# The last feed-forward block's first projection: seven block products per pair of hidden tiles instead of eight

## The chip, the cores and the metric

One core of a Trainium2 chip runs the whole kernel. The metric is the device time of one execution in microseconds (us). Times inside a profile count from the start of its span. The engines are TensorE (PE in the profile; its weight loads are PEld), VectorE (DVE), ScalarE (ACT), GpSimd (POOL) and SyncE (SP), which starts the DMAs.

## The reference

One inference step of a two-layer audio encoder: 512 new prompt frames and 8 streams of 16 frames, 640 columns in all, with 1024 features. Layer 0 is a convolution module and a feed-forward block, layer 1 attention and a feed-forward block. All is float32. What the change touches is the feed-forward block of layer 1:

```
def swiglu_ffn(h, g, w_in, w_out):
    a, b = jnp.split(rms_norm(h, g) @ w_in, 2, axis=-1)
    return h + (jax.nn.silu(a) * b) @ w_out
```

`w_in` is 1024 x 5632 (hidden size 2816, for `a` and for `b`), `w_out` is 2816 x 1024. A last `rms_norm` follows and gives the output.

## The kernel before

Features lie on the 128 partitions and frames along the columns. `h` holds 8 feature tiles (k = 0 to 7) of 640 columns; the columns are worked on in two groups, `GR`: 0 with 256 columns, 1 with 384. A float32 operand is split into a high part (ACT copies it, rounded) and a low part (DVE subtracts the high part), and each product takes three matmuls: high weight by high x, low weight by high x, high weight by low x (`mm3`, lines 161 to 163). Weights are split by `wsplit` (DMA at lines 125 and 130, ACT `whi` at 141, DVE or POOL `wlo` at 145), activations by `xsplit` (ACT at line 150, DVE at line 151).

The block in question is at the end of the program. `rms_late` multiplies `h` by the norm's gain (DVE, line 243) and splits the result; the norm's factor per column (`bc`) is worked out beside it (squares on ACT at 168, their sum on POOL at 184, column means on PE at 193, the power on POOL at 218, the spread over partitions on PE at 205, the copy on ACT at 250) and is multiplied in only after the projection. `ffn` then goes over the 22 hidden tiles in the three chunks of `F1` (9, 9 and 4). For each tile j, `ffn_in` loads 128 x 2048 weights (the tile of `a` and the tile of `b`) and runs for each column group two sums of 8 x 3 matmuls: 96 matmuls of 256 or 384 columns for a pair of tiles. Lines 278 to 281 multiply by `bc`, take the silu (ACT) and the product, and `xsplit` writes `hid`. After each chunk `ffn_out` adds that chunk's part of the second projection to `h` (DVE, line 291). In the last chunk of 4 tiles all of group 1's columns are done first and then all of group 0's, so that the final norm of group 1 (lines 876 to 886) runs beside the matmuls of group 0. Ahead of the block stands the last attention projection, `proj_o(3)`, whose results DVE adds to `h` at line 694.

The order on each engine is set by the framework's scheduler, which places the operations by its own estimate and by priorities (`tc.high_priority`); each engine then runs its row of instructions strictly in that order.

## Time and profile before

| what | value |
|---|---|
| median of 3 runs | 1572.6 us (1569.3 to 1572.96) |
| profiled execution, its own time | 1573.84 us |
| its span, first to last instruction | 1572.1 us |
| mean granted TensorE clock | 0.984 |
| PE busy | 1497.4 us, 95% of the span |
| DVE, ACT, POOL busy | 970.1, 605.0 and 396.8 us |

The profiled execution took 1.2 us more than the median, and its span is 1.7 us shorter than its own time. Busy times are sums over stages with different limits: the last stage, from about 1085 us to the end, is the one to read here. A row of a group gives the line, the engine and the operation, what it writes and reads, the shape, the count, busy time and mean duration of one, and the idle time ahead of it with the engine it waited for.

### The profile page before, as it was taken

To read this page: it belongs to the slowest core of one execution; us is meant where nothing else is said; L and a number is where in the kernel's file an instruction comes from. 1 tells how busy PE (TensorE), PEld (TensorE's weight loads), DVE (VectorE), ACT (ScalarE), POOL (GpSimd) and SP (SyncE) were. 2 spreads that over 40 slices of the span, in tenths; PEclk is the share of its full clock that TensorE was granted. 3 is DMA by queue.
4 is the path that set the end of the run, shared out by engine and by line. 5 is a ranking of instruction groups with operands and counts; after the bars stand their busy time and mean duration, and the time that the engine had idled before them with its cause. 6 is when DMAs were issued, how large, how long until landed. Compare 5 with 4: busy or idle time off the path is not lost.

```text
span 1572.1 us, 26820 instructions
## 1 busy us (share of the span) xinstructions
PE 1497.4 (95%) x10998; PEld 1426.5 (91%) x10998; DVE 970.1 (62%) x1781; ACT 605.0 (38%) x1064; POOL 396.8 (25%) x368
## 2 busy tenths in 40 slices
PE   5888998989999999999999999998999999999997
PEld 5878888888999999999987898876999999999997
DVE  6994999988545545456776668575744334443345
ACT  4544454545433323235654345442522112221223
POOL 6864568877501000004221111011300000000001
PEclk9999999999999999999999999998999999999999
DMA  7884344444412333434655554450121232212311
GB/s 238 233 241 125 126 129 147 153 166 145 148 57 81 121 124 117 148 114 131 222 180 168 174 190 153 155 194 28 64 72 58 70 103 79 81 46 76 108 54 67
DMA packets 58700, 199.98 MB, mean 127 GB/s; under 512 B 10193, under 2 KB 22737, under 8 KB 45777
## 3 DMA queue, kind: packets, MB, share of 16 engines
q1 hardware_dynamic: 58288, 197.96, 39.1%
q8 instruction: 86, 1.41, 0.4%
q10 hardware_dynamic: 288, 0.31, 0.1%
q14 instruction: 38, 0.30, 0.1%
HBM read 187.02 MB, written 11.22 MB: 126 GB/s over the span
## 4 chain that ended last, share of the span: by engine, by line
PE 74%; DVE 15%; POOL 3%; issue 3%; ACT 2%; DMA 2%; SPq 0%; POOLq 0%; ACTq 0%; DVEq 0%
PE mm L161 22%; PE mm L162 22%; PE mm L163 22%; DVE w L425 5%; DVE wlo L145 4%; PE w L780 1%; DVE xl L151 1%; DMA x<-sc 1%; PE am L765 1%; POOL y L405 1%; PE am L748 1%; ACT whi L141 1%; PE am L811 1%; PE mm L457 1%; DVE hid L151 1%
## 5 line engine op out<-in xcount | busy, mean ns | idle before, releaser
L162 PE MATMUL mm<-xh,wlo 128*128 128x256 f32 (+1 forms) x2048 | 633.7, 311 | 14.9 <-DVE wlo L145 14.5
L161 PE MATMUL mm<-xh,whi 128*128 128x256 f32 (+1 forms) x2048 | 630.2, 311 | 8.2 <-ACT xh L150 3.7
L163 PE MATMUL mm<-xl,whi 128*128 128x256 f32 (+1 forms) x2048 | 630.0, 310 | 0.8 <-DVE xl L151 0.6
L162 PEld LDWEIGHTS mm<-xh,wlo 128*128 128x128 f32 x2048 | 390.8, 191 | 18.1 <-DVE wlo L145 17.0
L161 PEld LDWEIGHTS mm<-xh,whi 128*128 128x128 f32 x2048 | 388.5, 191 | 13.1 <-ACT xh L150 6.7
L163 PEld LDWEIGHTS mm<-xl,whi 128*128 128x128 f32 x2048 | 388.8, 191 | 3.0 <-DVE xl L151 1.9
L141 ACT ACTIVATE whi<-raw 128x2048 fp32r<-128x2048 f32 (+3 forms) x140 | 235.1, 1682 | 331.9 <-PE mm L163 269.4
L145 DVE TENSOR_TENSOR wlo<-raw,whi 128x2048 fp32r<-128x2048 f32 (+6 forms) x140 | 262.3, 1876 | 77.6 <-ACT whi L141 76.2
L162 PE MATMUL mm<-hid,wlo 128*128 128x384 f32 (+1 forms) x704 | 215.7, 308 | 6.7 <-DVE wlo L145 6.7
L163 PE MATMUL mm<-hid,whi 128*128 128x384 f32 (+1 forms) x704 | 213.5, 306 | 0.1
L161 PE MATMUL mm<-hid,whi 128*128 128x384 f32 (+1 forms) x704 | 212.1, 306 | 0.0
L145 POOL TENSOR_TENSOR wlo<-raw,whi 128x1536 fp32r<-128x1536 f32 (+3 forms) x50 | 145.1, 2905 | 70.4 <-ACT whi L141 70.4
L280 DVE TENSOR_TENSOR t<-mm,bc 128x384 f32<-128x384 f32 x66 | 33.8, 513 | 186.5 <-PE mm L163 186.5
L162 PEld LDWEIGHTS mm<-hid,wlo 128*128 128x128 f32 x704 | 132.3, 188 | 8.1 <-DVE wlo L145 8.1
L163 PEld LDWEIGHTS mm<-hid,whi 128*128 128x128 f32 x704 | 131.8, 188 | 0.5 <-DVE hid L151 0.3
L161 PEld LDWEIGHTS mm<-hid,whi 128*128 128x128 f32 x704 | 131.2, 188 | 0.2
L218 POOL TENSOR_TENSOR rst<-rst,mhalf 128x2 f32<-128x2 f32 (+1 forms) x7 | 6.0, 864 | 447.4 <-DVE rst L214 447.4
L291 DVE TENSOR_TENSOR h<-mm,h 128x384 f32<-128x384 f32 (+1 forms) x112 | 53.8, 485 | 102.7 <-PE mm L163 102.5
L425 DVE SCALAR_TENSOR_TENSOR w<-gp,dwv,w 128x384 f32<-128x384 f32 x180 | 103.8, 611 | 0.8
L279 ACT ACTIVATE t<-t 128x384 f32<-128x384 f32 x66 | 32.3, 490 | 157.0 <-DVE t L278 157.0
L150 ACT ACTIVATE hid<-t 128x384 fp32r<-128x384 f32 (+1 forms) x88 | 40.7, 462 | 117.2 <-DVE t L281 83.4
L184 POOL TENSOR_TENSOR acc<-sq,sq 128x384 f32<-128x384 f32 (+1 forms) x9 | 9.2, 1025 | 267.2 <-ACT sq L168 267.1
(154 smaller groups left out, 1897.7 us busy)
## 6 DMA issues: line engine op xcount, KB each, us to landing
raw<-in_w_in SPq DMA_DIRECT2D x62, 1024.0 KB
raw<-in_w_pw SPq DMA_DIRECT2D x22, 1024.0 KB
raw<-in_w_out SPq DMA_DIRECT2D x24, 768.0 KB
cache<-in_ck SPq DMA_DIRECT2D x32, 512.0 KB
cache<-in_cv SPq DMA_DIRECT2D x32, 512.0 KB
raw<-in_w_out SPq DMA_DIRECT2D x16, 576.0 KB
raw<-in_w_kq SPq DMA_DIRECT2D x8, 1024.0 KB
x<-sc SPq DMA_DIRECT2D x16, 368.0 KB
```

The costliest lines, as they stand in the source:

```text
L141: nc.scalar.activation(out=hi[:, a:b], in_=raw[:, a:b], func=AF.Copy)
L145: eng.tensor_tensor(out=lo[:, a:b], in0=raw[:, a:b], in1=hi[:, a:b].bitcast(F32), op=ALU.subtract)
L150: nc.scalar.activation(out=hi, in_=src, func=AF.Copy)
L151: nc.vector.tensor_tensor(out=lo, in0=src, in1=hi.bitcast(F32), op=ALU.subtract)
L161: nc.tensor.matmul(ps, wh, xh, start=(i == 0), stop=False)
L162: nc.tensor.matmul(ps, wl, xh, start=False, stop=False)
L163: nc.tensor.matmul(ps, wh, xl, start=False, stop=(i == last))
L279: nc.scalar.activation(out=s[:, :n], in_=s[:, :n], func=AF.Silu)
L280: nc.vector.tensor_tensor(out=t[:, :n], in0=ps[1], in1=bc, op=ALU.mult)
L291: nc.vector.tensor_tensor(out=hp(g, m), in0=pt[:, :n], in1=hp(g, m), op=ALU.add)
L405: nc.gpsimd.tensor_tensor(out=y[g][:, c, :], in0=y[g][:, c, :], in1=pr[:, :n], op=ALU.add)
L425: nc.vector.scalar_tensor_tensor(out=dst, in0=src, scalar=wj, in1=dst, op0=ALU.mult, op1=ALU.add)
```

## The change

In all but the first three pairs of hidden tiles the first projection is done by a block scheme with seven products. The 640 columns are cut into two halves of 320 (`TH`), the 1024 features into two halves of four tiles. With `A11`, `A12` for the weights of `a` and `A21`, `A22` for those of `b`, and `B` for the four blocks of x, four sums of weights (S1 to S4) and four of x (T1 to T4) are formed, and seven products of 12 matmuls with 320 columns each give both halves of `a` and `b`: 84 matmuls for a pair. The products are accumulated in three banks (`pa`, `pb`, `pc`): a product is copied out by ACT (`u`, `v`) and added into another bank by DVE (in `m6`), and later products accumulate on top of that.

* The weight sums are formed in place in `raw`, 512 columns each, two on DVE and two on POOL (`WE = "vpvp"`). 3584 columns of weights are split for a pair instead of 2048.
* The x blocks must hold the norm's factor before they are summed, so ACT writes the gained x (`xg`), the first three pairs run plainly on it (`plain`, four sums of 24 matmuls with 320 columns), and meanwhile DVE multiplies the blocks by the factor (`bca`), forms T1 to T4 and, with ACT, splits all seven blocks into 1280 columns each (`put`). `B11` and `B21`, `B22` and `T4` take the places of the plain x, `B22` and `T4` only after the third pair's last matmuls.
* The pairs are interleaved: the first, fifth, sixth and second product of the next pair stand between the seventh, third and fourth of the present one.
* The chunks of the second projection are 6, 6, 5 and 5 tiles (each chunk: 8 output tiles of both column groups), and in each chunk the two column groups alternate. The second projection's arithmetic is as before.
* `proj_o(3)` works on column halves instead of the two groups. Elsewhere only buffers are merged or named anew: ahead of `proj_o(3)` the rows of all engines stand as they did, but for some places at the end of layer 0 and the start of attention, where a few neighbours swap.

In the whole program 228 matmuls fall away: 19 pairs times 12.

Three places in the rows of the engines, before and now. Names end in a number for the buffer. First DVE in the middle of the first projection. Before, the work for one pair of tiles: scaling, product and low part for both groups, and one split of weights.

```order
L278 TENSOR_TENSOR t_1749_13612<-mm_13562,bc_11627 128x384
L280 TENSOR_TENSOR t_1750_13613<-mm_13587,bc_11627 128x384
L281 TENSOR_TENSOR t_1750_13613<-t_1749_13612,t_1750_13613 128x384
L151 TENSOR_TENSOR hid_13310<-t_1750_13613,hid_13310 128x384
L278 TENSOR_TENSOR t_1753_13670<-mm_13620,bc_11696 128x256
L280 TENSOR_TENSOR t_1754_13671<-mm_13645,bc_11696 128x256
L281 TENSOR_TENSOR t_1754_13671<-t_1753_13670,t_1754_13671 128x256
L145 TENSOR_TENSOR wlo_13802<-raw_13800,whi_13801 128x2048
L151 TENSOR_TENSOR hid_13311<-t_1754_13671,hid_13311 128x256
```

Now, from the end of one pair's fourth product on: `t` is the gate product, `bk` and `wlo` the low parts of weights, `raw` the weight sums, `pb` and `pc` the additions in the banks, `acc` the copy-out after the seventh product.

```order
L907 TENSOR_TENSOR t_1694_13187<-t_1683_13095,pb_13068 128x320
L159 TENSOR_TENSOR bk_13224<-raw_13220,bk_13224 128x512
L159 TENSOR_TENSOR hc_12850<-t_1694_13187,hc_12850 128x320
L907 TENSOR_TENSOR raw_13220<-raw_13220 128x512
L907 TENSOR_TENSOR pb_13191<-pb_13191,acc_13115 128x320
L907 TENSOR_TENSOR pc_13143<-pb_13191,sq_13144 128x320
L159 TENSOR_TENSOR wlo_13346<-raw_13343,whi_13345 128x1024
L159 TENSOR_TENSOR wlo_13223<-raw_13220,whi_13222 128x1024
L907 TENSOR_TENSOR raw_13343<-raw_13343 128x512
L907 TENSOR_TENSOR acc_13264<-pb_13191,sq_13144 128x320
L159 TENSOR_TENSOR bk_13224<-raw_13220,bk_13224 128x1024
L907 TENSOR_TENSOR t_1706_13293<-t_1706_13293,acc_13264 128x320
```

Nine operations for a pair have become thirteen, and two of them write the banks on which the next products accumulate.

Second ACT, where the first pairs are under way. Before, from the norm's factor on (`bc` to the next weights):

```order
L250 ACTIVATE bc_11627<-w_1544_11593 128x384
L279 ACT_TABLE_LOAD
L279 ACTIVATE t_1586_11756<-t_1586_11756 128x384
L150 ACTIVATE hid_11698<-t_1587_11757 128x384
L141 ACTIVATE whi_11945<-raw_11944 128x2048
L250 ACTIVATE bc_11696<-w_1567_11664 128x256
L279 ACTIVATE t_1590_11814<-t_1590_11814 128x256
```

Now, some microseconds later, around the start of the products: `x0f`, `x1f` and `xe` are high parts of x blocks (here of `B21`, `B22` and T2), `whi_12055` the weights of the first pair that is done by products (its second half holds S1 and S2), `acc_12079` the copy of its first product.

```order
L158 ACTIVATE x0f<-xg 128x1280
L158 ACTIVATE hc_11563<-t_1564_11862 128x320
L158 ACTIVATE x1f<-xg 128x1280
L158 ACTIVATE whi_12139<-raw_12137 128x1024
L158 ACTIVATE xe<-tq 128x1280
L158 ACTIVATE hc_11563<-t_1568_11920 128x320
L158 ACTIVATE whi_12055<-raw_12053 128x1024
L936 ACTIVATE t_1574_11983<-t_1574_11983 128x320
L910 ACTIVATE acc_12079<-pa_12078 128x320
L936 ACTIVATE t_1578_12045<-t_1578_12045 128x320
L1029 ACTIVATE t_1589_12135<-pa_12078 128x320
```

The high part of S1 and S2 now stands behind `B22` and T2 in ACT's row.

Third DVE at the end of the program. Before, where group 1's sums of squares (`acc_15651`) end and group 0's begin:

```order
L291 TENSOR_TENSOR h<-mm_15522,h 128x384
L184 TENSOR_TENSOR acc_15651<-acc_15651,sq_15670 128x384
L291 TENSOR_TENSOR h<-mm_15536,h 128x256
L291 TENSOR_TENSOR h<-mm_15550,h 128x256
L184 TENSOR_TENSOR acc_15688<-sq_15686,sq_15689 128x256
L291 TENSOR_TENSOR h<-mm_15564,h 128x256
L214 TENSOR_SCALAR rst_15676<-w_1929_15648 128x3
```

Now:

```order
L192 TENSOR_TENSOR acc_15688<-acc_15688,sq_15704 128x384
L1067 TENSOR_TENSOR h<-pc_15630,h 128x256
L1067 TENSOR_TENSOR h<-pa_15647,h 128x384
L192 TENSOR_TENSOR acc_15688<-acc_15688,sq_15707 128x384
L1067 TENSOR_TENSOR h<-pb_15664,h 128x256
L192 TENSOR_TENSOR acc_15724<-sq_15722,sq_15725 128x256
L222 TENSOR_SCALAR rst_15713<-w_1942_15685 128x3
```

Before, five of group 0's eight tiles are still to be added when group 1's mean (`rst`) is taken; now the last tiles of both groups are added first, and group 0's sum begins behind them.

The diff, cut to what the steps speak of:

```
+HT = 320
...
+TG = (slice(0, 256), slice(256, 640))
+TH = (slice(0, HT), slice(HT, 2 * HT))
...
-F1 = ((0, 9), (9, 9), (18, 4))
+F1 = ((0, 6), (6, 6), (12, 5), (17, 5))
+CH = 6
+NPL = 3
+WE = "vpvp"
...
-        return (cst.tile([P, KT, n], F32R, tag=f"xh{g}", name=nm("xh")),
-                cst.tile([P, KT, n], F32R, tag=f"xl{g}", name=nm("xl")))
+        t = cst.tile([P, 2, KT, n], F32R, tag=f"x{g}", name=nm("x"))
+        return t[:, 0], t[:, 1]
...
-        for g in OG if r == NP // 2 - 1 else (0, 1):
-            g0, n = GR[g]
+        last = r == NP // 2 - 1
+        for c in TH if last else TG:
+            n = c.stop - c.start
             for m in range(KT):
-                pt = mmt()
+                pt = bank() if last else mmt()
                 mm3(pt[:, :n], [(wh[:, (k * 8 + m) * P:(k * 8 + m + 1) * P],
                                  wl[:, (k * 8 + m) * P:(k * 8 + m + 1) * P]) for k in range(2)],
-                    [(oT[2 * r + k][0][:, g0:g0 + n], oT[2 * r + k][1][:, g0:g0 + n])
-                     for k in range(2)])
-                nc.vector.tensor_tensor(out=hp(g, m), in0=pt[:, :n], in1=hp(g, m), op=ALU.add)
+                    [(oT[2 * r + k][0][:, c], oT[2 * r + k][1][:, c]) for k in range(2)])
+                nc.vector.tensor_tensor(out=h[:, m, c], in0=pt[:, :n], in1=h[:, m, c],
+                                        op=ALU.add)
...
+    w2 = hf.enter_context(tc.tile_pool(name="w2f", bufs=1, space=PSUM, **tr))
+    mms = ExitStack()
+    hf.push(mms)
+    mm = mms.enter_context(tc.tile_pool(name="mm2", bufs=2, space=PSUM, **tr))
...
-    xs = {g: rms_late(g, V_NFFN + KT) for g in FG}
-    ffn({0: hpf, 1: hpf}, w_in1, w_out1, xs, FG, F1, 0, (1, 0), max(ch for _, ch in F1), (0, HPAD))
+    xc = [(xb[2 * i], xb[2 * i + 1]) for i in range(7)]
+    blk = [[xg[q][:, :, c] for c in TH] for q in range(2)]
+    raw_slot = [[xc[B11], xc[T4]], [xc[B21], xc[B22]]]
...
+    def plain(j, jj, q, wts):
+        wh, wl = wts
+        c = TH[q]
+        ps = []
+        for ab in range(2):
+            pt = bank()
+            o = [(8 * ab + (k + 4 * ab) % 8) * P for k in range(KT)]
+            mm3(pt[:, :HT], [(wh[:, i:i + P], wl[:, i:i + P]) for i in o],
+                [(raw_slot[k // 4][q][0][:, k % 4, :], raw_slot[k // 4][q][1][:, k % 4, :])
+                 for k in range(KT)])
+            ps.append(pt[:, :HT])
+        with tc.high_priority(offset=HP):
+            gate(ps[0], ps[1], hids[0], jj, c)
+
+    def prod(ps, w, x, first):
+        wh, wl = w
+        xh, xl = x
+        for k in range(4):
+            c = slice(k * P, (k + 1) * P)
+            for i, (a, b) in enumerate(((wh, xh), (wl, xh), (wh, xl))):
+                nc.tensor.matmul(ps, a[:, c], b[:, k, :], start=(first and k == 0 and i == 0),
+                                 stop=(k == 3 and i == 2), skip_group_check=not first)
...
+        def prep(u, a22=None):
+            r = wp.tile([P, 2048], F32, tag="raw", name=nm("raw"))
+            nc.sync.dma_start(r, w_in1[u.j])
+            hi = wp.tile([P, 2048], F32R, tag="whi", name=nm("whi"))
+            lo = wp.tile([P, 2048], F32R, tag="wlo", name=nm("wlo"))
+            if a22 is None:
+                bk = wf.tile([P, 2 * 1536], F32R, tag="bk", name=nm("bk"))
+                a22 = bk[:, 0:512], bk[:, 1536:2048]
+            else:
+                bk = None
+            q = u.q = [r[:, 512 * i:512 * i + 512] for i in range(4)]
+            u.r = r[:, 0:1024]
+            with tc.high_priority(offset=HP):
+                xsplit(r[:, 0:1024], hi[:, 0:1024], lo[:, 0:1024])
+                xsplit(q[2], *a22)
+                add(WE[0], q[0], q[0], q[3], ALU.subtract)
+                add(WE[1], q[3], q[3], q[2])
+                add(WE[2], q[2], q[2], q[0], ALU.subtract)
+                xsplit(r[:, 1024:2048], hi[:, 1024:2048], lo[:, 1024:2048])
+                add(WE[3], q[1], q[1], q[2], ALU.subtract)
+            u.a11, u.a12, u.s2, u.s1 = [quarter(hi, lo, i) for i in range(4)]
+            u.a22 = a22
...
+        def prep_back(u, bk=None):
+            if bk is None:
+                bk = wf.tile([P, 2 * 1536], F32R, tag="bk", name=nm("bk"))
+            bh, bl = bk[:, 512:1536], bk[:, 2048:3072]
+            with tc.high_priority(offset=HP):
+                xsplit(u.r, bh, bl)
+            u.s3, u.s4 = [quarter(bh, bl, i) for i in range(2)]
+
+        def m1(u):
+            u.pa = bank("pa")[:, 0:HT]
+            u.u = tmp("acc")
+            prod(u.pa, u.a11, xc[B11], True)
+            with tc.high_priority(offset=2 * HP):
+                copy(u.u, u.pa)
+
+        def m5(u):
+            u.pc = bank("pc")[:, 0:HT]
+            u.v = tmp("sq")
+            prod(u.pc, u.s1, xc[T1], True)
+            with tc.high_priority(offset=2 * HP):
+                copy(u.v, u.pc)
+
+        def m6(u):
+            u.pb = bank("pb")[:, 0:HT]
+            prod(u.pb, u.s2, xc[T2], True)
+            with tc.high_priority(offset=2 * HP):
+                add("v", u.pb, u.pb, u.u)
+                add("v", u.pc, u.pb, u.v)
+
+        def m2(u):
+            prod(u.pa, u.a12, xc[B21], False)
+            with tc.high_priority(offset=2 * HP):
+                u.s = tmp("t1")
+                nc.scalar.activation(out=u.s, in_=u.pa, func=AF.Silu)
+
+        def m7(u):
+            prod(u.pb, u.s3, xc[T3], False)
+            with tc.high_priority(offset=2 * HP):
+                u.c = tmp("acc")
+                add("v", u.c, u.pb, u.v)
+
+        def m3(u):
+            prod(u.pc, u.s4, xc[B22], False)
+            with tc.high_priority(offset=HP):
+                s = tmp("t3")
+                nc.scalar.activation(out=s, in_=u.pc, func=AF.Silu)
+                add("v", s, s, u.c, ALU.mult)
+                xsplit(s, u.hid[:, 0, u.jj, TH[1]], u.hid[:, 1, u.jj, TH[1]])
+
+        def m4(u):
+            prod(u.pb, u.a22, xc[T4], False)
+            with tc.high_priority(offset=HP):
+                t = tmp("t2")
+                add("v", t, u.s, u.pb, ALU.mult)
+                xsplit(t, u.hid[:, 0, u.jj, TH[0]], u.hid[:, 1, u.jj, TH[0]])
+
+    def outs(c):
+        j0, ch = F1[c]
+        hid = hids[c]
+        for m0 in range(0, KT, 2):
+            src = w_out1[m0:m0 + 2, :, j0 * P:(j0 + ch) * P].rearrange("m p c -> p m c")
+            wh, wl = wsplit(src, ch * 2, P, parts=2)
+            for m in range(m0, m0 + 2):
+                b = (m - m0) * ch
+                for t in (TH[1], TH[0]) if m == 0 else (TG[1], TG[0]):
+                    n = t.stop - t.start
+                    pt = bank()
+                    mm3(pt[:, :n], [(wh[:, (b + k) * P:(b + k + 1) * P],
+                                     wl[:, (b + k) * P:(b + k + 1) * P]) for k in range(ch)],
+                        [(hid[:, 0, k, t], hid[:, 1, k, t]) for k in range(ch)])
+                    with tc.high_priority(offset=HP):
+                        nc.vector.tensor_tensor(out=h[:, m, t], in0=pt[:, :n], in1=h[:, m, t],
+                                                op=ALU.add)
+
+    for q in range(2):
+        for k in range(KT):
+            x = xg[k // 4][:, k % 4, TH[q]]
+            nc.scalar.activation(out=x, in_=h[:, k, TH[q]], func=AF.Copy,
+                                 scale=col(V_NFFN + KT, k))
+            if k % 2:
+                hi, lo = raw_slot[k // 4][q]
+                k0 = k % 4 - 1
+                xsplit(blk[k // 4][q][:, k0:k0 + 2, :], hi[:, k0:k0 + 2, :], lo[:, k0:k0 + 2, :])
+    for g in range(2):
+        g0, n = GR[g]
+        bc, _ = rstd_bc([hp(g, k) for k in range(KT)], n, SQ, CUT)
+        nc.scalar.activation(out=bca[:, g0:g0 + n], in_=bc, func=AF.Copy)
...
+    (b11, b12), (b21, b22) = blk
+    for j in range(NPL):
+        wts = wsplit(w_in1[j], 16, P)
+        for q in range(2):
+            plain(j, j, q, wts)
+            if j == NPL - 1 and q == 0:
+                with tc.high_priority(offset=HP):
+                    put(B11, b11)
+                    put(B21, b21)
+        if j == 0:
+            for x, c in ((b12, 1), (b11, 0), (b22, 1), (b21, 0)):
+                add("v", x, x, bcast(TH[c]), ALU.mult)
+            add("v", tq, b12, b11, ALU.subtract)
+            put(T1, tq)
+            add("v", tq, b22, tq, ALU.subtract)
+            put(T2, tq)
+            add("v", b12, b22, b12, ALU.subtract)
+            put(T3, b12)
+            add("v", tq, b21, tq, ALU.subtract)
+    u = Unit(NPL, hids[0], NPL)
+    u.prep((hids[0][:, 0, CH - 1, 0:512], hids[0][:, 1, CH - 1, 0:512]))
+    with tc.high_priority(offset=HP):
+        put(B22, b22)
+        put(T4, tq)
...
+    u.prep_back()
+    for f in (u.m1, u.m5, u.m6, u.m2):
+        f()
+    for j in range(NPL, FT):
+        c, jj = where[j]
+        w = None
+        if j + 1 < FT:
+            w = Unit(j + 1, hids[c], where[j + 1][1])
+            w.prep()
+        if w:
+            w.m1()
+        u.m7()
+        if w:
+            w.m5()
+        u.m3()
+        u.m4()
+        if w:
+            w.m6()
+            w.m2()
+        if jj == F1[c][1] - 1:
+            outs(c)
+            if w:
+                hids.append(new_hid())
+                w.hid = hids[-1]
+        u = w
...
-        ffn.append(np.stack([t[:FT], t[FT:]], axis=2).reshape(FT, P, 2048))
+        b = t[FT:]
+        if l:
+            b = b.reshape(FT, P, 2, 4 * P)[:, :, ::-1]
+        ffn.append(np.stack([t[:FT].reshape(FT, P, -1), b.reshape(FT, P, -1)],
+                            axis=2).reshape(FT, P, 2048))
```

90 lines of the change are left out of this document (79 added, 11 removed).

## The prediction

> **What bounds the kernel now.** I read the page first (busy time by engine), then stretches of the last stage, then the groups of that stage, and at its two ends the timeline.
>
> ```profile
> span 1572.1 us, 26820 instructions
> PE 1497.4 (95%) x10998; PEld 1426.5 (91%) x10998; DVE 970.1 (62%) x1781; ACT 605.0 (38%) x1064; POOL 396.8 (25%) x368
> ```
>
> PE is busy for 95% of the span, but a busy PE is not yet PE at its peak. The stretches settle it; columns are the stretch, its length, busy time and instructions of PE, PEld, DVE, ACT and POOL, granted clock, DMA share, GB/s.
>
> ```profile
> 1130.00:1550.00 420.00, 420.00 (x2920) 420.00 (x2919) 169.94 (x248) 101.30 (x131) 0.00 (x0) 1.00 0.22 71
> 1160.00:1270.00 110.00, 110.00 (x768) 110.00 (x767) 42.98 (x64) 25.01 (x32) 0.00 (x0) 1.00 0.20 63
> ```
>
> For 420 us PE never waits, at full clock, while DVE is busy 40% and ACT 24%. In the second row, which is first projection alone, 768 matmuls take 110 us: 0.1432 us each, at a mean width of 320 columns (half have 256, half 384). So the block is bound by the number of matmul columns, and a matmul that falls away there is worth its 0.1432 us, as long as DVE, ACT and POOL stay hidden. What they need comes from the groups of 1130 to 1573:
>
> ```profile
> L145 DVE TENSOR_TENSOR wlo<-raw,whi 128x2048 fp32r<-128x2048 f32 x21 | 48.1, 2292 | 22.1 <-ACT whi L141 22.1
> L141 ACT ACTIVATE whi<-raw 128x2048 fp32r<-128x2048 f32 x21 | 40.2, 1916 | 55.3 <-PE mm L163 55.3
> L145 DVE TENSOR_TENSOR wlo<-raw,whi 128x1152 fp32r<-128x1152 f32 x16 | 21.7, 1358 | 10.4 <-ACT whi L141 10.4
> L141 ACT ACTIVATE whi<-raw 128x1152 fp32r<-128x1152 f32 x16 | 18.7, 1167 | 85.4 <-PE mm L163 72.8 <-issue 12.6
> L280 DVE TENSOR_TENSOR t<-mm,bc 128x384 f32<-128x384 f32 x20 | 11.1, 557 | 66.7 <-PE mm L163 66.7
> L150 ACT ACTIVATE hid<-t 128x384 fp32r<-128x384 f32 x20 | 10.5, 526 | 79.5 <-DVE t L281 79.5
> L280 DVE TENSOR_TENSOR t<-mm,bc 128x256 f32<-128x256 f32 x21 | 8.9, 424 | 48.2 <-PE mm L163 48.2
> L150 ACT ACTIVATE hid<-t 128x256 fp32r<-128x256 f32 x21 | 8.4, 401 | 0.0
> L886 POOL TENSOR_TENSOR h<-h,b 128x384 f32<-128x384 f32 x4 | 4.1, 1056 | 3.5 <-ACT b L876 3.5
> ```
>
> DVE takes 2292 ns for 2048 columns and 1358 for 1152: 1.04 ns a column and 158 ns fixed, so 692, 1225 and 1492 ns for 512, 1024 and 1280; 320 columns lie midway between 424 and 557, at 490. ACT in the same way: 632, 1060 and 1274 ns, and 464 for 320. Operations that wait for nothing overlap a little:
>
> ```profile
> 1123.38 0.42 DVE L278 TENSOR_TENSOR t<-mm,bc 128x256 f32<-128x256 f32 x1
> 1123.71 0.41 DVE L280 TENSOR_TENSOR t<-mm,bc 128x256 f32<-128x256 f32 x1
> 1124.05 0.55 DVE L278 TENSOR_TENSOR t<-mm,bc 128x384 f32<-128x384 f32 x1
> ```
>
> They start 0.33 us apart and last 0.42, so a dense row of DVE costs 0.08 us less for each.
>
> **The change, term by term.** *Matmuls.* 19 pairs by 12 matmuls of 320 columns: 228 x 0.1432 = 32.7 us less. A pair takes 12.03 us of PE instead of 13.75. The second projection has the same columns in the same two widths, so it costs what it did; its weights (now 1536 or 1280 columns for two output tiles) and additions stay hidden as they are now, and a fourth chunk adds 16 additions of 0.49 us under PE.
>
> *DVE and ACT for a pair.* DVE: low parts 3 x 1.225 + 0.692, two weight sums 2 x 0.692, seven operations of 320 columns x 0.490: 9.2 us, less 13 x 0.08 is 8.1. ACT: 3 x 1.06 + 0.63 + 6 x 0.464 = 6.6 us. POOL: two sums of 512, near the row of 384 columns at 1.06 us, so some 1.4 us each. All are below 12.03. But POOL and DVE get in each other's way, as two groups from 340 to 700 us show, where POOL splits weights:
>
> ```profile
> L151 DVE TENSOR_TENSOR hid<-t,hid 128x256 fp32r<-128x256 f32 x10 | 15.7, 1568 | 1.4 <-ACT hid L150 1.4
> L276 DVE TENSOR_TENSOR t<-t,mm 128x256 f32<-128x256 f32 x9 | 3.7, 414 | 3.8 <-PE mm L163 3.8
> ```
>
> With both inputs in SBUF, 256 columns take 1568 ns there, against about 420 without POOL; with one input in PSUM (the `mm`) they keep their 414. So each POOL sum can hold up one DVE operation for up to 1.4 us: 10.9 us for a pair at worst, still hidden. The additions in the banks have one input in PSUM and should keep their time.
>
> *Loads.* SP still loads 1 MB for each pair, and 16 pieces of 640 or 768 KB for the second projection. `raw` is held longer, until the sums are split; with two buffers a load has some 8 of a pair's 12 us, and at the 348 GB/s of the row below it needs 3:
>
> ```profile
> 1106.00:1108.00 2.00, 2.00 (x13) 2.00 (x12) 2.00 (x3) 0.94 (x2) 1.45 (x2) 1.00 0.87 348
> ```
>
> I cost it at nothing; if that cover went, it would be PE's wait for the first product's weights.
>
> *The tight link.* Between the sixth product of a pair and its seventh, on the same bank, DVE must do two additions one after the other. From the end of the pair before's fourth product DVE has, in its row: gate product, low part of weights, low part of the product, weight sum, and then the two additions: about 0.25 us until it starts, then 0.49 + 0.75 + 0.40 + 0.60 + 0.55 + 0.50 = 3.5. PE has 11 + 15 matmuls to do meanwhile: 26 x 0.1432 = 3.7 us. So it just fits; I take 2.5 us in all for the 19 pairs (some 0.85 for the first ones, little for the rest), with 0 and 20 as ends (1 us for each).
>
> *Start of the block.* Now PE loses time twice when the second half of `proj_o(3)` and the first x are due, because DVE is late; the granted clock then halves.
>
> ```profile
> 1096.59 0.44 PE L161 MATMUL mm<-ohi,whi 128*128 128x384 f32 x1 [1.21 <-DVE h L694]
> 1101.20 0.41 PE L161 MATMUL mm<-xh,whi 128*128 128x384 f32 x1 [2.23 <-DVE h L694]
> 1101.80:1105.24 3.44, 3.44 (x12) 3.44 (x12) 3.22 (x3) 2.01 (x5) 2.53 (x1) 0.51 0.00 0
> 1121.94 0.39 ACT L250 ACTIVATE bc<-w 128x256 f32<-128x256 f32 x1 [0.80 <-PE w L205]
> ```
>
> 1.21 + 2.23 us of waiting, and 3.44 us with the clock at 0.51, of which half, 1.7, is lost: 5.1 us. In the change the gain goes to ACT, DVE has only 8 additions of 0.49 us beside 4 low parts of 640 columns for the first half, and the second half of `proj_o(3)` gives 48 x 0.143 = 6.9 us for it, and six banks instead of two let PE run ahead: I count 4.5 us saved (between 5.1 and 2).
>
> *Start of the products.* PE comes to the fifth product (S1) 3 x 96 + 12 + 13 matmuls after its first plain one, 44.8 us later. DVE can't form the blocks before the norm's factor is there; now the later group's factor is ready at 1122.33, 21 us after the first matmul, and I take 20.5, since the order of sums is much the same. From then until S1's low part DVE's row holds 13 operations of 1280 columns, 3 of 1024, 2 of 512 and 19 of 320: 13 x 1.41 + 3 x 1.15 + 2 x 0.61 + 19 x 0.41 = 30.8 us, and two waits for POOL's sums, 1.5. So S1 is ready at about 52.8, 8 us late. Ahead of that PE is stopped by ACT already: `B22` may be split only behind the third pair's last matmul, and B22, 1024 of weights, T2, a product and S1/S2 take 1.27 + 1.06 + 1.27 + 0.46 + 1.06 = 5.1 us there, against 1.7 us of the first product; that stop of 3.3 us lies within the 8. The seventh product then waits another 1.2 for T4 and the additions. With a stop of over 2.23 us I charge the clock's 1.7 again, less the part that falls into waiting: 1.3. Sum 10.5 us, between 4 (if DVE catches up while PE runs the plain pairs) and 18 (if the factor comes late).
>
> [...]
>
> *End.* Now the last matmul starts at 1560.66, and 11.2 us remain behind its end.
>
> ```profile
> 1560.66 0.28 PE L163 MATMUL mm<-hid,whi 128*128 128x256 f32 x1
> 1558.12 4.10 POOL L886 TENSOR_TENSOR h<-h,b 128x384 f32<-128x384 f32 x4 [3.54 <-ACT b L876]
> 1563.19 0.58 PE L193 MATMUL w<-onec,acc 128*128 128x1 f32 x4 [2.25 <-DVE acc L184]
> 1565.61 3.22 DVE L881 SCALAR_TENSOR_TENSOR h<-h,vec,w 128x256 f32<-128x256 f32 x8 [1.58 <-PE w L205]
> ```
>
> Group 1's scaling on POOL (4.10 us) starts 2.5 us before that matmul, beside group 0's tiles. In the change the last tiles of both groups come last: behind the last matmul stand one addition (0.4), six of group 0's sums at about 0.45 (they go at the pace of ACT's squares), four scalings of group 1 on DVE (2.3) and the last sum, while POOL begins its four scalings at about 4.0 and is free for group 0's power at 8.1; power and spread take until 9.6, the eight scalings 3.22, and the output another 3.3: 16.2, or 5.0 more (ends 2 and 7).
>
> **Sum.** -32.7 + 2.5 - 4.5 + 10.5 + 5.0 = -19.2 us. The profiled execution (1573.84, 1.2 above the median) would come to 1554.6, a median run of 1572.6 to 1553.4. I say 1553.
>
> **Rivals.**
>
> * *The tight link breaks.* If DVE is late by 0.6 us more for each of 18 pairs, because an operation ahead of the two additions waits for POOL or ACT, 11 us come on top: 1564. For it: the row is strict and the margin 0.2 us. Against: POOL's sums start behind the weight sum, next to the additions, which keep their 414 ns.
> * *The starts are smooth.* If DVE is done with the blocks in time, the start of the products costs 2 instead of 10.5: 1545. For it: half of DVE's row is placed freely under 41 us of plain matmuls. Against: 30.8 us of it must come behind the factor.
> * *The start of the products is longer.* Two of POOL's sums of squares (384 columns) that met a split of 2048 columns took 1.96 us each, four later ones (256 columns) 1.05, in the rows below. If half of the 14 are slow, the factor comes 6 us later: 1559. Against: much of that sum is done while DVE has little else.
>
> ```profile
> 1102.71 3.92 POOL L184 TENSOR_TENSOR acc<-acc,sq 128x384 f32<-128x384 f32 x2 [3.13 <-ACT sq L168]
> 1111.18 4.18 POOL L184 TENSOR_TENSOR acc<-acc,sq 128x256 f32<-128x256 f32 x4
> ```
>
> * *Slower: the link stops PE long enough for the clock.* If each of 18 links lost 2.2 us, as long as the gap above that was followed by half the clock, it would cost 2.2 + 1.7 = 3.9 each, 70 us in place of the 2.5: 1621. It decides from 1.2 us a link on, where the 21.7 us that the other terms leave are gone. For it: nothing hides the link but 15 matmuls. Against: 1.2 us more is a third of what DVE does in it. [...]
>
> **Chances.** The forecast as summed (1548 to 1558) 55%, the link 17%, smooth starts 12%, a longer start 9%, slower 4%, and 3% that several of these leave it within 0.3%, about 4.7 us, which is what a measurement here can tell from no change. The range takes in the smooth starts and the broken link, 1541 to 1567. Faster 0.93, same 0.03, slower 0.04.
>
> **What would show it.** In the middle of a chunk PE should be busy without gaps, 84 matmuls in about 12.0 us for a pair, DVE at two thirds to three quarters, and the clock at 1.00. Wrong would be idle time of PE put down to DVE ahead of the products that use `bk` weights and the bank `pb`. The start of products should show PE waiting first for ACT (weights S1 and S2), then for DVE, 8 to 10 us in all, once. At the first plain pair the gaps of 1.21 and 2.23 us should be gone. At the end, some 16 us should lie behind the last matmul. The forecast fails if the link loses over half a microsecond for each pair, or if matmuls of 320 columns do not follow each other at 0.143 us.

## The result and the profile after

| | before | after |
|---|---|---|
| median, first comparison (4 runs each) | 1572.8 us (1569.3 to 1573.8) | 1553.0 us (1551.2 to 1556.7) |
| ratio, first comparison | | 0.9881 [0.9858, 0.9905] |
| ratio, second comparison (8 and 4 runs) | | 0.9892 [0.9877, 0.9907] |
| span of the profiled execution | 1572.1 us | 1549.4 us |
| predicted | | 1553, range 1541 to 1567 |

The time is the one predicted: 1.2% less. The sum hides that three of its five terms were off by 3 to 8 us, in both directions. The profiled executions lie 22.7 us apart, 3 more than the medians.

The first part of the page of after, busy time and instructions by engine:

```profile
span 1549.4 us, 26575 instructions
PE 1470.8 (95%) x10770; PEld 1399.3 (90%) x10770; DVE 1045.6 (67%) x1862; ACT 662.0 (43%) x1172; POOL 447.2 (29%) x406
```

There are 10998 - 10770 = 228 matmuls fewer. Three stretches of after (columns as in the prediction); the first holds products alone, the other two the second projection of the first and of the second chunk:

```profile
1350.00:1384.00 34.00, 34.00 (x234) 34.00 (x233) 22.15 (x33) 14.61 (x26) 6.39 (x5) 1.00 0.17 62
...
1209.23:1229.87 20.64, 20.64 (x146) 20.64 (x145) 10.65 (x14) 4.67 (x4) 2.59 (x2) 1.00 0.17 52
1314.75:1346.55 31.80, 31.80 (x218) 31.80 (x217) 14.96 (x20) 6.80 (x6) 2.58 (x2) 1.00 0.21 69
```

PE is full at full clock, with DVE busy 65%, ACT 43%, POOL 19%: the cover held. But a pair takes longer than 84 x 0.1432 = 12.03 us. The timeline of after has the first matmul of the seventh product in two pairs that follow each other:

```profile
1243.95 0.31 PE L961 MATMUL pb<-xe,bk 128*128 128x320 f32 x1
...
1256.27 0.60 PE L961 MATMUL pb<-xe,bk 128*128 128x320 f32 x3
```

That is 12.32 us for 84 matmuls with nothing between them: 0.1467 us each. 3.4 ns seem little, but there are some 2000 of these matmuls. The second chunk's row is slow in itself: 31.80 us for 216 matmuls, where the first chunk takes 20.64 for 144. In a second profile of the same kernel (experiment 10) the second chunk's 216 took 30.95, at the first chunk's pace, so this comes with the execution and not with the kernel:

```profile
1317.84:1348.79 30.95, 30.95 (x218) 30.95 (x217) 14.98 (x20) 6.79 (x6) 2.59 (x2) 1.00 0.21 69
```

**Start of the block.** A common landmark is the first of four matmuls at the end of attention, the same instruction in both kernels, in the timeline of before:

```profile
1039.27 0.82 PE L765 MATMUL am<-PT,vt 128*64 128x384 f32 x4
```

and of after, with the first matmul of the first plain pair:

```profile
1039.59 0.82 PE L776 MATMUL am<-PT,vt 128*64 128x384 f32 x4
...
1091.50 0.31 PE L169 MATMUL pb<-x0f,whi 128*128 128x320 f32 x1
```

Up to the landmark the two executions are 0.3 us apart. From it to the first plain matmul after takes 51.9 us, before 61.9 (1101.20, a row of the prediction). The first matmul of `proj_o(3)` splits this stretch in two, in the timeline of before and of after:

```profile
1082.26 0.38 PE L161 MATMUL mm<-ohi,whi 128*128 128x256 f32 x1 [0.70 <-ACT ohi L150]
```

```profile
1076.66 0.41 PE L169 MATMUL pa<-ohi,whi 128*128 128x320 f32 x1
```

From the landmark to it are 43.0 us before and 37.1 after, from it to the first plain matmul 18.9 and 14.8. Behind that matmul, before also lost 1.7 us to the half clock.

**Start of the products.** The waits of TensorE from 1080 to 1150 and from 1150 to 1250 (what waited, for whom: us in total, times, longest), and behind them the stretch with the worst of it:

```profile
PE pa L961 <- ACT whi L158: 2.2, 1, 2.2
PE pc L961 <- DVE wlo L159: 1.8, 1, 1.8
...
PE pb L961 <- DVE pc L907: 1.4, 1, 1.4
```

```profile
1135.00:1145.00 10.00, 6.93 (x34) 6.04 (x32) 10.00 (x13) 5.84 (x8) 1.29 (x1) 0.83 0.01 3
```

First ACT, then DVE, then the link: the order that the prediction gave. 5.4 us of waiting, and 1.7 us of work lost to the clock, 0.83 over 10 us being 3.4 us at half: 7.1. DVE's row shows why, with the first operation behind the norm's factor and the low part of S1:

```profile
1113.38 0.49 DVE L907 TENSOR_TENSOR t<-pb,bca 128x320 f32<-128x320 f32 x1 [1.59 <-ACT bca L1082]
...
1144.59 1.21 DVE L159 TENSOR_TENSOR wlo<-raw,whi 128x1024 fp32r<-128x1024 f32 x1
```

S1 is ready at 1145.80, 54.3 us after the first plain matmul (forecast 52.8), with 32.4 us behind the factor (forecast 30.8 + 1.5). The plain pairs ahead of it kept TensorE busy without a gap, but longer than the 41.2 us (288 x 0.1432) of the forecast:

```profile
1091.50:1135.98 44.48, 44.48 (x310) 44.37 (x308) 34.33 (x36) 21.22 (x30) 10.91 (x10) 1.00 0.14 48
```

**End.** The timeline of after, PE, DVE and POOL:

```profile
1532.07 0.28 PE L171 MATMUL pb<-hc,whi 128*128 128x256 f32 x1
1539.58 1.01 PE L201 MATMUL w<-onec,acc 128*128 128x1 f32 x4 [3.84 <-DVE acc L192]
...
1536.32 2.18 DVE L1160 SCALAR_TENSOR_TENSOR h<-h,vec,w 128x384 f32<-128x384 f32 x4
1538.42 1.11 DVE L192 TENSOR_TENSOR acc<-acc,sq 128x256 f32<-128x256 f32 x1
...
1536.34 4.03 POOL L1165 TENSOR_TENSOR h<-h,bca 128x384 f32<-128x384 f32 x4 [1.94 <-ACT bca L1155]
```

From the last matmul's end (1532.07 + 0.28) to the end of the span are 17.1 us, 5.9 more than before. Group 0's last sum stands on DVE behind group 1's four scalings, and takes 1.11 us instead of 0.42 beside POOL.

### The profile page after: what moved, and what is told of

Read it like the earlier page. It is cut to its first block, busy times and chain, and to the rows that moved or that the text cites. A ratio compares the mean times of both kernels' runs of the same rounds, so it can differ in the third digit from the quotient of the medians.

```text
span 1549.4 us, 26575 instructions
## 1 busy us (share of the span) xinstructions
PE 1470.8 (95%) x10770; PEld 1399.3 (90%) x10770; DVE 1045.6 (67%) x1862; ACT 662.0 (43%) x1172; POOL 447.2 (29%) x406
## 4 chain that ended last, share of the span: by engine, by line
PE 72%; DVE 14%; DMA 3%; issue 3%; ACT 3%; POOL 3%; SPq 0%; POOLq 0%; ACTq 0%; DVEq 0%
PE mm L169 13%; PE mm L171 13%; PE mm L170 12%; PE pb L961 6%; DVE w L433 5%; PE pc L961 4%; PE pa L961 4%; DVE wlo L153 3%; PE pb L169 1%; PE pc L169 1%; PE pb L170 1%; PE pb L171 1%; PE pc L171 1%; PE pc L170 1%; PE pa L171 1%
## 5 line engine op out<-in xcount | busy, mean ns | idle before, releaser
L170 PE MATMUL mm<-x,wlo 128*128 128x256 f32 (+1 forms) x1344 | 416.7, 312 | 13.5 <-DVE wlo L153 11.4
L169 PE MATMUL mm<-x,whi 128*128 128x256 f32 (+1 forms) x1344 | 412.9, 312 | 6.7 <-ACT x L158 3.7
L171 PE MATMUL mm<-x,whi 128*128 128x256 f32 (+1 forms) x1344 | 412.8, 311 | 0.7 <-DVE x L159 0.3
L170 PEld LDWEIGHTS mm<-x,wlo 128*128 128x128 f32 x1344 | 256.3, 191 | 17.0 <-DVE wlo L153 14.0
L169 PEld LDWEIGHTS mm<-x,whi 128*128 128x128 f32 x1344 | 254.0, 191 | 11.6 <-ACT x L158 4.2
L171 PEld LDWEIGHTS mm<-x,whi 128*128 128x128 f32 x1344 | 255.0, 191 | 3.0 <-DVE x L159 1.8
L170 PE MATMUL mm<-hid,wlo 128*128 128x256 f32 (+1 forms) x352 | 107.6, 308 | 6.9 <-DVE wlo L153 6.9
L171 PE MATMUL mm<-hid,whi 128*128 128x256 f32 (+1 forms) x352 | 105.7, 307 | 0.8 <-DVE hid L159 0.7
L169 PE MATMUL mm<-hid,whi 128*128 128x256 f32 (+1 forms) x352 | 104.4, 306 | 0.0
L170 PEld LDWEIGHTS mm<-hid,wlo 128*128 128x128 f32 x352 | 66.0, 188 | 8.1 <-DVE wlo L153 8.1
L413 POOL TENSOR_TENSOR y<-y,cvt 128x256 f32<-128x256 f32 (+1 forms) x60 | 69.1, 1152 | 6.3 <-ACT cvt L412 4.0
L171 PEld LDWEIGHTS mm<-hid,whi 128*128 128x128 f32 x352 | 65.7, 188 | 1.2 <-DVE hid L159 1.2
L169 PEld LDWEIGHTS mm<-hid,whi 128*128 128x128 f32 x352 | 65.1, 188 | 0.3 <-ACT hid L158 0.2
L961 PE MATMUL pa<-x0f,whi 128*128 128x320 f32 x228 | 61.3, 315 | 2.2 <-ACT whi L158 2.2
```

The source lines that it names most:

```text
L169: nc.tensor.matmul(ps, wh, xh, start=(i == 0), stop=False)
L170: nc.tensor.matmul(ps, wl, xh, start=False, stop=False)
L171: nc.tensor.matmul(ps, wh, xl, start=False, stop=(i == last))
L413: nc.gpsimd.tensor_tensor(out=y[g][:, c, :], in0=y[g][:, c, :], in1=pr[:, :n], op=ALU.add)
L961: nc.tensor.matmul(ps, a[:, c], b[:, k, :], start=(first and k == 0 and i == 0), stop=(k == 3 and i == 2), skip_group_check=not first)
```

## Experiments

Ratios are to the kernel before, in runs on the same chip, with their 95% interval. The changed kernel had 0.9881 and 0.9892.

**1. A fourth plain pair.**

```diff
-NPL = 3
+NPL = 4
```

> Four plain pairs instead of three ahead of the products. A fourth plain pair costs 96 x 0.1467 = 14.1 us of TensorE instead of 84 x 0.1467 = 12.3, 1.8 us more. At the start of the products the changed kernel loses 2.2 + 1.8 + 1.4 us of waiting and about 1.7 us to the half clock, 7.1 in all. Theory (the blocks are late on DVE): 14 us more of plain matmuls cover the waits for DVE (1.8 and 1.4) and with them the clock goes too; the wait of 2.2 us for ACT stays, because it stands behind the last plain pair whatever its number: 1.8 - 4.9 = 3.1 us faster than the changed kernel, about 1550. Rival (each of the stops hangs on the last plain pair, not on the time since the norm): nothing goes, 1.8 us slower, about 1555.

Measured: 1547.3 us, 0.9859 [0.9839, 0.9878]. The waits of TensorE at the start of the products are now

```profile
PE pa L961 <- ACT whi L158: 0.8, 1, 0.8
PE pa L961 <- ACT acc L910: 0.5, 1, 0.5
```

So 5.4 us of waiting became 1.3 and the half clock there is gone: 5.8 us won for the 1.8 that the pair costs. The waits for DVE went, as the theory had it; the wait for ACT shrank too, against the theory. So most of these stops hang on the time since the norm's factor, and not on the last plain pair.

**2, 3, 4. The end: order and bank.** Experiment 2 gives the last chunk four tiles, with the weights of all eight outputs in two buffers, and runs group 1 through all outputs ahead of group 0. Experiment 3 adds another PSUM tile for group 1's last norm; experiment 4 has that tile alone.

```diff
-F1 = ((0, 6), (6, 6), (12, 5), (17, 5))
+F1 = ((0, 6), (6, 6), (12, 6), (18, 4))
...
+        if c == len(F1) - 1:
+            wts = []
+            for m0 in (0, 4):
+                src = w_out1[m0:m0 + 4, :, j0 * P:(j0 + ch) * P].rearrange("m p c -> p m c")
+                wts.append(wsplit(src, ch * 4, P, parts=4))
+            for t in (TG[1], TG[0]):
+                n = t.stop - t.start
+                for m in range(KT):
...
```

```diff
-    mms.close()
-    w2 = hf.enter_context(tc.tile_pool(name="w2g", bufs=2, space=PSUM, **tr))
     bcs = {}
     with tc.high_priority(offset=HP):
         for g in (1, 0):
+            if g == 0:
+                mms.close()
+                w2 = hf.enter_context(tc.tile_pool(name="w2g", bufs=2, space=PSUM, **tr))
```

> Chunks of 6, 6, 6 and 4 tiles; the last one holds the weights of all eight output tiles in two buffers and runs group 1 through all eight outputs first, then group 0. Theory (the end is 5.9 us longer because both groups' last tiles come last): the work behind the last matmul goes back from 17.1 to about 11.2 us, 1553 - 5.9 = 1547. Rival (the end is set by POOL and DVE in any order): no change, 1553. A price to look for: the second buffer of weights can be split only behind the last pair's products; if it is late TensorE stops, up to 2 us.

> As the run with a last chunk of four tiles and group 1 through all outputs first, and besides the last norm of group 1 has its PSUM tile in the buffer that the block's first norm used, so it needn't wait until the products' banks are empty. In the run with the order alone 14.95 us lay behind the last matmul (17.05 in the changed kernel), and group 1's column means stood behind all matmuls on TensorE although its sums were ready at 1531.6, 7 us ahead of the last matmul. Theory (order and bank together make the long end): some 11.2 us remain, as before the change: 5.9 us less than the changed kernel, 1547. Rival (the end is DVE's and POOL's chain of group 0): 14 to 15 us remain, 1550. Price to look for: the norm's small matmuls now stand between group 0's and can stop TensorE, up to 2 us.

> The changed kernel with the other PSUM tile for group 1's last norm and nothing else; both groups' last tiles still come last. Theory (it takes order and bank): group 1's last tile is done only 15 x 0.1136 = 1.7 us ahead of the last matmul, so at most 1.7 us fall away behind it: 15.4 to 17 us remain, 1551.5 to 1553. Rival (the bank alone made the end long): about 11 to 12 us remain, 1548.

Measured, with two stretches of each profile: from the last matmul's end to the end of the span, and from the first plain matmul to the end of the span:

| | behind the last matmul | from the first plain matmul | time | ratio |
|---|---|---|---|---|
| changed kernel | 17.1 us | 457.9 | 1553.0 | 0.9881 [0.9858, 0.9905] |
| order alone | 15.0 | 455.8 | 1554.6 | 0.9901 [0.9874, 0.9928] |
| bank alone | 17.9 | 458.8 | 1554.1 | 0.9898 [0.9882, 0.9913] |
| both | 13.3 | 455.6 | 1551.1 | 0.9873 [0.9851, 0.9895] |

In the run with the order alone (timeline, PE) group 1's means do stand behind the last matmul:

```profile
1538.46 0.28 PE L171 MATMUL pb<-hc,whi 128*128 128x256 f32 x1
1538.58 0.72 PE L201 MATMUL w<-onec,acc 128*128 128x1 f32 x6
```

Behind the last matmul order and bank together took away 3.7 of the 5.9 us. But not all of this is gain: with the bank, 12 small matmuls of group 1's norm stand among group 0's, ahead of the last matmul (timeline of both together, PE):

```profile
1531.61 0.72 PE L201 MATMUL w<-onec,acc 128*128 128x1 f32 x6
...
1535.69 0.83 PE L213 MATMUL w<-ident,rst 128*128 128x128 f32 x6
```

From the first plain matmul to the end of the span, order alone saves 2.1 us and both together 2.3: the bank mostly moved work to an earlier place. The times alone can't show effects of this size, their intervals overlap, and each trace is a single one. Why this end is still longer than the one of before is seen in the last experiment's trace.

**5. Widths.** The second projection with other cuts, the outputs 6 and 7 as before.

```diff
+def cut(n):
+    return slice(n, 640), slice(0, n)
+OW = [cut(n) for n in (320, 320, 288, 288, 304, 312, 256, 256)]
...
-                for t in (TH[1], TH[0]) if m == 0 else (TG[1], TG[0]):
+                for t in OW[m]:
```

> The second projection's halves are cut at other columns, by output tile: 0 and 1 at 320/320, 2 and 3 at 288/352, 4 at 304/336, 5 at 312/328, 6 and 7 at 256/384 as before. In the changed kernel matmuls of 320 columns follow each other at 0.1467 us, while 256 and 384 columns take 0.1134 and 0.1732, of which the mean is 0.1433. Theory (a width's own time, not on the line between 256 and 384): 320 columns take 0.1467 here too, right beside rows of 0.1134 and 0.1732; what 288, 304, 312, 328, 336 and 352 take, this run shows (on the line it would be 0.1284, 0.1358, 0.1396, 0.1470, 0.1508 and 0.1583). If only 320 is off, 0.4 us slower, 1553.5; if all are off by 3.4 ns, 660 x 3.4 ns = 2.2 us slower, 1555. Rival (it is the products, their three banks or their weights, that slow the matmuls): 320 columns in the second projection follow at 0.143 us.

Measured: 1554.2 us, 0.9899 [0.9877, 0.9921]. The first matmul of each output tile of the first chunk, 18 matmuls a tile, in its timeline:

```profile
1207.04 0.32 PE L176 MATMUL pb<-hc,whi 128*128 128x352 f32 x1
1209.92 0.29 PE L176 MATMUL pc<-hc,whi 128*128 128x288 f32 x1
1212.31 0.32 PE L176 MATMUL pa<-hc,whi 128*128 128x336 f32 x1
1215.07 0.30 PE L176 MATMUL pb<-hc,whi 128*128 128x304 f32 x1
1217.56 0.31 PE L176 MATMUL pc<-hc,whi 128*128 128x328 f32 x1
1220.25 0.30 PE L176 MATMUL pa<-hc,whi 128*128 128x312 f32 x1
1222.83 0.34 PE L176 MATMUL pb<-hc,whi 128*128 128x384 f32 x1
1225.97 0.28 PE L176 MATMUL pc<-hc,whi 128*128 128x256 f32 x1
1228.03 0.33 PE L176 MATMUL pa<-hc,whi 128*128 128x384 f32 x1
```

From start to start: 352 + 288 columns take 2.88 + 2.39 = 5.27 us, 336 + 304 take 2.76 + 2.49 = 5.25, 328 + 312 take 2.69 + 2.58 = 5.27, and 384 + 256 take 3.14 + 2.06 = 5.20. Two tiles of 320 take 2.64 each in this run, 5.28. For the same 640 columns every cut but 256/384 costs 1 to 1.5% more here; against the 5.16 that 256/384 took in the first chunk of after (20.64 / 4) it is 5 to 7 ns for two matmuls. So the time belongs to the width, not to the products, their banks or their weights; the rival falls. That only 320 is off falls too. The time's difference (1.2 us in the medians) is too small to be told by runs.

**6. A longer link.**

```diff
+                for _ in range(6):
+                    add("v", tq[:, 0, :], u.pb, u.u)
                 add("v", u.pb, u.pb, u.u)
                 add("v", u.pc, u.pb, u.v)
```

> Six further additions of 320 columns (0.40 us each in a dense row) ahead of the two additions between the sixth product and the seventh, 2.4 us more for DVE in each of the 19 links; they write what nothing reads. Theory (the link has slack, as the trace shows: in one pair the second addition ends at 1254.55 and the seventh product starts at 1256.27, 1.7 us later, with no idle time on TensorE): 2.4 - 1.7 = 0.7 us lost in each, 19 x 0.7 = 13 us, about 1566. Rival 1 (the prediction's margin of 0.2 us): 2.2 us in each, 42 us, about 1595. Rival 2 (DVE's spare time, not the link, takes it up): no change, 1553. If 0.7 us of idling every 12 us is enough to bring the granted clock down, up to 1.7 us more for each: 1598, with a clock clearly below 1.00 in the block.

Measured: 1571.9 us, 1.0006 [0.9991, 1.002], some 19 us slower than the changed kernel, between the two theories. The waits of TensorE from 1160 to 1550, the four largest:

```profile
PE pb L961 <- DVE pc L907: 4.3, 3, 2.2
PE pc L961 <- ACT whi L158: 3.3, 4, 2.1
PE pa L170 <- DVE wlo L153: 1.6, 3, 0.8
PE pa L169 <- ACT whi L149: 1.2, 1, 1.2
```

All waits in this stretch are 12.6 us, and only 4.3 of them stand in the link; most others are for weights that came late. The extra additions did not stay together: weight splits stand between them in DVE's row. As a measure of the link's slack the run is inconclusive. The trace of after gives it directly. Its DVE's second addition and the seventh product behind it, in two pairs:

```profile
1254.06 0.49 DVE L907 TENSOR_TENSOR pc<-pb,sq 128x320 f32<-128x320 f32 x1
...
1292.88 0.50 DVE L907 TENSOR_TENSOR pc<-pb,sq 128x320 f32<-128x320 f32 x1
...
1293.53 0.68 PE L961 MATMUL pb<-xe,bk 128*128 128x320 f32 x3
```

In the first pair the addition ends 1.72 us ahead of its product (1256.27, above), in the second 0.15 us. Of 19 links 9 have less than half a microsecond, 6 about 1.75, and 4 have matmuls of the second projection between. The first of them waits 1.4 us (counted with the start of the products). At seven of the others the matmuls around the link come 0.13 us late, 0.9 us together; at the rest nothing is lost.

**7. Two banks for the last `proj_o`.**

```diff
-            tag = ("pa", "pb", "pc")[banks[0] % 3]
+            tag = ("pa", "pb", "pc")[0 if banks[0] < 16 else banks[0] % 3]
```

> The last proj_o runs through two PSUM banks, as before the change, instead of six; all else as in the changed kernel. Theory (the six banks let TensorE run ahead, so DVE's late additions no longer stop it): the waits of about 1.2 and 2.2 us come back, with the half clock's 1.7: 5 us slower, 1558. Rival (that ACT scales x and DVE has eight additions and four low parts in the half took the waits away): no wait over 0.5 us there, 1553.

Measured: 1558.6 us, 0.9931 [0.9907, 0.9956], the size expected and not the place. The timeline (ACT, PE) and a stretch:

```profile
1105.61 1.89 ACT L149 ACTIVATE whi<-raw 128x2048 fp32r<-128x2048 f32 x1
...
1107.56 0.41 PE L169 MATMUL pc<-x0f,whi 128*128 128x320 f32 x1 [2.72 <-ACT whi L149]
```

```profile
1100.00:1120.00 20.00, 16.36 (x93) 15.61 (x92) 10.56 (x12) 9.93 (x18) 7.79 (x8) 0.83 0.14 53
```

TensorE doesn't stop in `proj_o`: from 1087 on it fills the waits with the first pair's first half. But `proj_o` then ends at 1104.8, and ACT, which takes its work in order, splits the next weights behind x's second half: a stop of 2.7 us, another of 0.7, and 6.8 us at half clock ((1 - 0.83) x 2 x 20). In this run the banks matter because with six of them the second half of x becomes ready earlier; the stops of `proj_o` itself were filled with other matmuls.

**8. No products.** All 22 pairs as the first three.

```diff
-    for j in range(NPL):
...
     for c, (j0, ch) in enumerate(F1):
+        if c:
+            hids.append(new_hid())
         for jj in range(ch):
+            wts = wsplit(w_in1[j0 + jj], 16, P)
+            for q in range(2):
+                plain(j0 + jj, jj, q, wts, hids[c])
+        outs(c)
```

> The changed kernel without the products and their sums: all 22 pairs as the first three, with halves of 320 columns and six banks; start and end of the block as in the changed kernel. Theory (320 columns take 0.1467 us, the start of the products costs 7.0, the links 1.5): 19 x 12 x 0.1467 = 33.4 us more, 8.5 less, so 24.9 slower than the changed kernel, 1578, and some 5 us slower than the kernel before, since 22 x 96 matmuls are 3.4 ns longer each (7.1 us) and the end is longer by 6, against 8 saved at the start. Rival (the prediction's own terms, 32.7 for the matmuls, 10.5 and 2.5 against it): 19.7 slower, 1573, level with the kernel before. If the products slow something that the trace doesn't show (SBUF or PSUM traffic), their removal gives less than 24.9.

Measured: 1579.2 us, 1.0058 [1.0038, 1.0078]: 26.1 us more than the changed kernel in the same comparison ((1.0058 - 0.9892) x 1570.8), against 24.9 expected and 19.7 by the prediction's terms. In the profiles the stretch from the first plain matmul to the end of the span is 481.0 us, 23.1 more than in the changed kernel, so that the difference is clear, but not to the microsecond. The products are worth more than the whole gain; what surrounds them, the halves of 320 and the longer end, costs 8 to 9 us against the kernel before.

**9. The kernel before once more, for its profile.** Nothing is changed.

> The kernel before, unchanged, for a second profile. Its first profile had the clock at half for 10.2 us at the end of the attention stage (from 1071.2 on); kernels with the changed block had there 0, 6.8, 3.4, 0, 10.2, 0, 0, 10.2 and 10.2 us, though all of them run the same instructions up to that place. Theory (it is a matter of chance and costs up to some 3.7 us): the second profile of the kernel before has 0, 3.4, 6.8 or 10.2 us as it happens, and the time from the attention's end to the first pair's first matmul follows it. Rival (the kernel before always has it, and the change takes it away): 10.2 again.

Measured: 1572.8 us. The stretch from 1070 to 1082, the end of attention and the first tiles of `proj_o`, in the first profile of before, in this one, in after, and in the changed kernel run again:

```profile
1070.00:1082.00 12.00, 9.31 (x67) 4.58 (x63) 2.58 (x9) 1.87 (x6) 0.00 (x0) 0.57 0.27 88
```

```profile
1070.00:1082.00 12.00, 9.98 (x68) 5.22 (x68) 2.25 (x8) 2.07 (x6) 0.00 (x0) 0.57 0.28 88
```

```profile
1070.00:1082.00 12.00, 10.14 (x94) 7.42 (x95) 4.85 (x14) 4.88 (x13) 0.74 (x1) 1.00 0.24 89
```

```profile
1070.00:1082.00 12.00, 9.98 (x73) 5.51 (x74) 3.05 (x10) 2.07 (x6) 0.00 (x0) 0.72 0.25 88
```

The clock there is 0.57, 0.57, 1.00 and 0.72, so 10.3, 10.3, 0 and 6.7 us at half. In the 12 profiles of kernels with the changed block it was none four times, 3.4 and 6.8 twice each, 10.2 four times. Their time from the landmark to the first plain matmul follows it: 51.9 to 52.8 us without, 52.9 and 53.5 with 3.4, 55.2 and 55.6 with 6.8, 55.5 to 56.1 with 10.2 (two banks left aside); before has 61.9 and 61.5. So some 3.9 us between the first two profiles hang on the clock there (the mean of the last group, 55.8, less 51.9). For the changed kernel this is chance. Two of two for the kernel before (a chance of one in nine, if it drew alike) doesn't tell whether it always pays; that stays open.

**10. A version that beats both.** Four plain pairs, order and bank of the end together, beside the changed kernel.

> Four plain pairs, the last chunk of four tiles with group 1 first, and group 1's norm in the free bank. If the parts add: 3.3 us (measured for four plain pairs against the changed kernel by the ratios to the kernel before, 0.9859 against 0.9881, of 1570) and 5.9 us less: 1553 - 9.2 = 1544. If the end stays long: 1550. If the fourth plain pair's gain was chance: 1547.

> The changed kernel, unchanged, beside the next one: 1553, ratio to the kernel before 0.988.

> Four plain pairs, a last chunk of four tiles with group 1 first, and group 1's norm in the free bank, beside the changed kernel. By the traces the fourth plain pair is worth 3.6 us and the end 4.1 (12.95 instead of 17.08 us behind the last matmul): 7.7 us less than the changed kernel, ratio to the kernel before 0.983. Rival (the first comparison, 0.9866, was not low by chance): 3 us less than the changed kernel.

Measured: 1548.0 us, 0.9866 [0.9851, 0.9881] the first time, 1548.9 us, 0.9863 [0.9848, 0.9877] the second, where the changed kernel beside it had 1553.8 us, 0.9892 [0.9877, 0.9907]. It is 4.9 us faster than the changed kernel and 1.4% faster than the kernel before. The 7.7 expected is not reached: the four times of each (1547.8 to 1549.4 and 1552.0 to 1554.0) lie at most 6.1 apart. The fourth plain pair alone had as good a ratio (0.9859). That the end adds to it, and less than expected, is shown by the traces alone: from the first plain matmul to the end of the span the changed kernel takes 457.9 and 457.5 us in its two profiles, the fourth plain pair alone 452.1, this version 450.5 and 450.8. So the end adds some 1.5 us, though only 12.9 us instead of 17.1 lie behind the last matmul; the norm's small matmuls have moved ahead of it. Its timeline (PE, DVE), first comparison:

```profile
1533.18 0.28 PE L171 MATMUL pc<-hc,whi 128*128 128x256 f32 x1
1537.10 0.60 PE L201 MATMUL w<-onec,acc 128*128 128x1 f32 x4 [3.65 <-DVE acc L192]
...
1532.86 2.19 DVE L1179 SCALAR_TENSOR_TENSOR h<-h,vec,w 128x384 f32<-128x384 f32 x4
1534.97 0.42 DVE L1070 TENSOR_TENSOR h<-pc,h 128x256 f32<-128x256 f32 x1
```

Group 1's four scalings stand on DVE ahead of group 0's last addition, though its bank was full at 1533.46. That addition comes 1.5 us late, of the 1.8 by which this end still exceeds the one of before.

## Why the prediction was right, point by point

The two first profiles, term by term:

| term | predicted | in the traces |
|---|---|---|
| matmuls | -32.7 us | -24.8 |
| tight link | +2.5 | +0.9 |
| start of the block | -4.5 | -11.7 |
| start of the products | +10.5 | +7.1 |
| end | +5.0 | +5.9 |
| all else | 0 | -0.1 |
| sum | -19.2 | -22.7 |

- **Matmuls: the mis-sized term.** The step that failed is "0.1432 us each, at a mean width of 320 columns": a mean over rows of 256 and 384 columns was taken for the time of 320. At 0.1467, 19 pairs save 19 x (13.75 - 12.32) = 27.1; against that, the plain pairs' 288 matmuls cost 1.0 more, the second projection's tiles of 320 columns 0.45 (the prediction took its widths for unchanged, but each chunk's first output tile is cut at 320), and the second chunk, whose 256 and 384 columns ran 2.7% slower than the first's in this execution, 0.8. The prediction had named the time of 320 columns as a way to fail, and its profile had rows of 256 and 384 only.
- **Tight link.** Right in kind: 0.9 us, or 2.3 with the first link's wait, which is counted at the start of the products. The additions in the banks kept their 0.49 us, also the 11 of 18 that had a POOL sum beside them. The margin of 0.2 us fits 9 of 19 pairs; in others the scheduler puts the additions earlier in DVE's row. "The link breaks" did not happen.
- **Start of the block.** Right in sign, too small. From `proj_o(3)`'s first matmul on, 4.1 us are saved, and the 1.7 of the half clock behind it: 5.8, where the forecast said 4.5 and at most 5.1. It had counted the two long waits and the clock. The other 5.9 us lie ahead of `proj_o(3)`, where the prediction counted nothing. Of these some 3.9 go with the half clock at the end of attention, in part chance; 0.7 is the wait for ACT ahead of `proj_o(3)`'s first matmul, which the changed kernel doesn't have; the rest stays open. Experiment 7 puts the six banks at 6 to 8 us (0.9931 against 0.9892 and 0.9881, with intervals as wide as that difference), since with two the second half of x comes later too.
- **Start of the products.** The stops came in the order forecast, S1 1.5 us later than forecast. Yet the stops for ACT and for S1 were 4.0 us together (2.2 and 1.8) instead of 8, because TensorE itself came later to S1. The plain pairs took 44.5 us instead of 41.2: 1.0 by the width, and 1.9 by 20 small matmuls of the norm that stand among them (lines 201 and 213) and that the prediction left out. The 26 matmuls between the two stops took 5.6 us, half of them at half clock, where the prediction had 25 in 3.6. The run with four plain pairs agrees: with 14 us more of work for TensorE the waits for DVE are gone.
- **End.** Right within a microsecond: the one missing is the last sum (1.11 instead of 0.42) and the means behind it (1.01 for four small matmuls instead of 0.58). POOL was free 8.0 us behind the last matmul, as forecast (8.1), but it was this sum on DVE that held up group 0's power, by another half microsecond.
- **The rivals.** None took place. The forecast's total held because the matmuls' miss of 7.9 us one way met 7.2 at the block's start and 3.4 at the products' start the other way. The range was wide enough for each alone, and this is luck rather than precision.
- **The clock.** The half clock came behind a wait of 2.2 us (0.50 from 1139 to 1142 us, 3.4 us in all). In four profiles (the changed kernel once more, order alone, order and bank, widths) it did not come at all, though the same matmuls took as long there (17.15 to 17.18 us against 17.16, last section), so that the waits were no shorter in sum. The charge of 1.3 us for it was thus a matter of chance, and the total did not hang on it (last section).
